# An encoder block on one Trainium2 core: values and output gate computed as eight pairs by seven products, x split tile by tile, row squares, and a hand-written order up to the first pair

## The chip, the cores and the metric

The kernel runs on one core of a Trainium2 chip. The time is the device time of one execution in microseconds (us); the number given for a kernel is the median of several runs. The trace that is quoted comes from one further execution under the hardware profiler.

## What is computed

One trunk layer of a hybrid encoder, in float32, for 2048 positions of width 1024. Only the first part matters here:

```python
xn = rms_norm(h, ln_mix_g)                 # h = x, (2048, 1024)
proj = xn @ w_in                           # (2048, 2512): q k v o | gates cq ckv kr
q_pre, k_pre = proj[:, 0:512], proj[:, 512:1024]
v_pre, o_pre = proj[:, 1024:1536], proj[:, 1536:2048]
rest = proj[:, 2048:2512]                  # 16 gates, 256 cq, 128 ckv, 64 kr
qk = silu(dwconv3_centred(q_pre | k_pre))  # along the 2048 positions
y_a = sigmoid(o_pre) * rms_norm(mlstm(q, k, v_pre, gates))
y_b = mla(rms_norm(cq), rms_norm(ckv), rope(kr))
h = h + concat(y_a, y_b) @ w_out           # then a gated MLP and an embedding gate
```

The row factor of the first norm, 1/sqrt(mean(x*x)+eps), is applied to the products and not to x; the gain is multiplied into the weights.

## The kernel before

Each float32 product is made of three matmuls on "fp32r" parts. An operand is split into a high part (a cast on ScalarE, ACT) and a low part (operand minus high part, on VectorE, DVE; `split`, L117), and a product is low*high + high*low + high*high (`mm3`, L131). A matmul of 128 rows by 512 columns over 1024 inputs is thus 8 blocks of 128 inputs times 3, 24 matmuls.

`in_proj` (L176) does the projections in three stages, and fills `x`-tiles, sixteen places of 16 KB per partition that hold the split x for all of them.

- **Rest** (the last 464 columns). For each of 16 tiles of 128 positions: load the tile of x (already turned, so that inputs lie on partitions), split it into its place (`split_x`), square it (ACT, L231), add the squares on DVE (L233, L234) and sum over partitions by two small matmuls with a column of ones (L237); GpSimd (POOL) raises that to -1/2 (L240), which gives the tile's row factor `rcol`. Then come 24 matmuls of 464 columns (`nat`), and in `rest` the results are scaled, normed and turned by the rotary table on DVE and ACT, and stored; two tiles later `turn_rest` transposes them on TensorE (PE, L281) and ACT copies the result out (L283).
- **Values and output gate.** Weights for 512 columns are loaded and split, then 16 tiles of 24 matmuls of 512 columns; the same again for the gate (L324 to L342). `gates()` is a generator of small steps, one of which is taken after each tile.
- **q and k** (`block`, L379): eight groups of 128 columns, four blocks of 512 positions each, 24 matmuls a block. The x parts are already in their places. A second generator, `side` (`absorb`, `q_up`), is advanced by `pump` three or four times a block, 0.986 steps a call. In this stage the order on PE is that of the program (`manual_schedule`); all other orders are made by a scheduler that knows costs.

Later stages already use pairs: two tiles of the left operand are taken together, both operands are cut into 2 by 2 blocks, and seven products of half the depth (12 matmuls each) take the place of eight (Winograd's form). `prep_a` and `prep_b` make the left sides of a pair from two loaded tiles: A11 and A12 (one split of 1024 columns), A22 (one of 512), four sums and differences of 512 on DVE, and two more splits of 1024 for S1, S3 and S2, S4. `OPX` names the places of the right sides B11, T1, T2, B21, T3, T4, B22.

Places in on-chip memory are named tags with one buffer each (`at`): a new tile under a tag waits until every reader of the old one is done. PSUM tags: `sc` has four banks, `tr` two, `pv` (the transposed rest tiles) one, `ml` one. Loads and stores are issued in order by one engine (SP).

Of the kernel before, what the change touches and what calls it, by code (L numbers as in the profile page):

```python
# [19 lines left out]
P = 128  # L20
S = 2048
# [15 lines left out]
LAG_T, LAG_X, LAG_R = 1, 2, 2  # L37
# [23 lines left out]
class Block:  # L61
# [114 lines left out]
    def in_proj(self):  # L176
        nc, d = self.nc, self.d
        xh = [[self.at(f"x{4 * c + 2 * f}", [P, 4, 512], F32R, f"xh{c}{f}") for f in range(2)] for c in range(4)]
        xl = [[self.at(f"x{4 * c + 2 * f + 1}", [P, 4, 512], F32R, f"xl{c}{f}") for f in range(2)] for c in range(4)]
        wrot, rrot, trot, srot = _rot("w", (*range(9), 13)), _rot("w", range(9, 13)), _rot("t", range(4)), _rot("s", range(3))  # L180
        w_in = d["w_in"][0].rearrange("(a b p) c -> a p b c", b=2, p=P)

        def load_w(c0, n, before=None):

            out, raws = [], []

            def load(k2, parts=1):
                raw = self.at(next(rrot), [P, 2, 512], name="wraw")
                for i in range(parts):
                    bs = slice(2 * i // parts, 2 * (i + 1) // parts)  # L190
                    nc.sync.dma_start(raw[:, bs, :n], w_in[k2, :, bs, c0:c0 + n])
                raws.append(raw)
                return raw

            if before:
                load(0, 2)
                before(0)
                load(1, 2)
                before(1)
                load(2)  # L200
                load(3)
            for k2 in range(KT // 2):
                if k2 == len(raws):
                    load(k2)
                raw = raws[k2]
                for b in range(2):
                    w = self.at(next(wrot), [P, 2, 512], F32R, "wsp")
                    self.split_g(raw[:, b, :n], gcol[:, 2 * k2 + b:2 * k2 + b + 1], w[:, 0, :n], w[:, 1, :n])
                    out.append(w)
            return out  # L210

        def nat(st, ws, n):
            ps = self.bank()
            c, o = st // 4, (st % 4) * P
            for kt in range(KT):
                f, k = divmod(kt, 4)
                self.mm3(ps[:, :n], xh[c][f][:, k, o:o + P], xl[c][f][:, k, o:o + P],
                         ws[kt][:, 0, :n], ws[kt][:, 1, :n], kt == 0, kt == KT - 1)
            return ps

        def load_x(st):

            t = self.at(next(rrot) if st else "u2", [P, KT, P], name="x_t")
            if st:
                nc.sync.dma_start(t, d["x_turned"][:, :, st * P:(st + 1) * P])
            return t

        def ssq_x(st, x_t):

            sq = self.at("w13", [P, KT, P], name="x_sq")  # L230
            nc.scalar.activation(sq, x_t, AF.Square)  # L231
            ss = self.at("t7", [P, 4, P], name="x_ss")
            nc.vector.tensor_tensor(ss, sq[:, 0:4], sq[:, 4:8], op=ALU.add)  # L233
            nc.vector.tensor_tensor(ss[:, 0:2], ss[:, 0:2], ss[:, 2:4], op=ALU.add)  # L234
            ps = self.pml.tile([P, 4], F32, name="ssp", tag="ml")
            for i in range(2):
                nc.tensor.matmul(ps, ss[:, i], ones, start=i == 0, stop=i == 1)  # L237
            t = self.stat(1, "rsm")
            nc.vector.tensor_scalar(t, ps[:, 0:1], 1.0 / D, EPS, op0=ALU.mult, op1=ALU.add)
            nc.gpsimd.tensor_tensor(rcol[:, st:st + 1], t, self.nhalf[:, :1], op=ALU.pow)  # L240

        def split_x(st, x_t):
            c, o = st // 4, (st % 4) * P
            for f in range(2):
                self.split(x_t[:, 4 * f:4 * f + 4], xh[c][f][:, :, o:o + P], xl[c][f][:, :, o:o + P])


        def rest(st):
            ps = nat(st, ws, NREST)
            rx = rcol[:, st:st + 1]  # L250
# [7 lines left out]
            cos, sin, tt = sc[:, 0], sc[:, 1], sc[:, 2:6]  # L258
# [5 lines left out]
            r = self.rsq(ssq, 2, 1.0)  # L264
            nc.vector.scalar_tensor_tensor(nn[:, 0:256], rs[:, 0:256], r[:, 0:1], gn[:, 0:256], op0=ALU.mult, op1=ALU.mult)
            nc.vector.scalar_tensor_tensor(nn[:, 256:384], rs[:, 256:384], r[:, 1:2], gn[:, 256:384], op0=ALU.mult, op1=ALU.mult)
            nc.sync.dma_start(self.vv_d[:, st], nn[:, 256:384])
            x1, x2 = rs[:, 384:416], rs[:, 416:448]
            nc.vector.tensor_tensor(tt[:, 0, :], x1, cos, op=ALU.mult)
            nc.vector.tensor_tensor(tt[:, 1, :], x2, sin, op=ALU.mult)  # L270
            nc.vector.tensor_tensor(tt[:, 2, :], x2, cos, op=ALU.mult)
            nc.vector.tensor_tensor(tt[:, 3, :], x1, sin, op=ALU.mult)
            nc.vector.tensor_tensor(nn[:, 384:416], tt[:, 0, :], tt[:, 1, :], op=ALU.subtract)
            nc.vector.tensor_tensor(nn[:, 416:448], tt[:, 2, :], tt[:, 3, :], op=ALU.add)
            nc.vector.tensor_copy(nn[:, 448:512], nn[:, 384:448])
            return nn

        def turn_rest(st, nn):
            pt = self.ppv.tile([P, 4, P], F32, name="rtp", tag="pv")
            for j in range(4):  # L280
                nc.tensor.transpose(pt[:, j, :], nn[:, j * P:(j + 1) * P], self.ident)  # L281
            rt = self.at(f"u{st % 2}", [P, 4, P], name="rt")
            nc.scalar.copy(rt, pt)  # L283
# [3 lines left out]
        nc.sync.dma_start(gcol, d["g_turned"])  # L287
# [3 lines left out]
        nq, xq = {}, {}  # L291

        xq[0] = load_x(0)

        def first(f):

            fs = slice(4 * f, 4 * f + 4)
            if f < 2:
                nc.sync.dma_start(xq[0][:, fs], d["x_turned"][:, fs, 0:P])
                self.split(xq[0][:, fs], xh[0][f][:, :, 0:P], xl[0][f][:, :, 0:P])  # L300

        ws = load_w(OFF_R, NREST, first)
        for st in range(NT + LAG_X):
            if st + 1 < NT:
                xq[st + 1] = load_x(st + 1)
            if st == 0:
                gn = self.at("t5", [P, 384], name="gn")
                self.row_bcast(gn[:, 0:256], d["q_norm_g"][0], 256)
                self.row_bcast(gn[:, 256:384], d["kv_norm_g"][0], 128)
                bg = self.row_bcast(self.cst.tile([P, 16], F32, name="bg"), d["b_gates"][0], 16)  # L310
            if 1 <= st < NT:
                split_x(st, xq[st])
            if 0 <= st - 1 < NT:
                ssq_x(st - 1, xq.pop(st - 1))
            if 0 <= st - LAG_X < NT:
                nq[st - LAG_X] = rest(st - LAG_X)
            if 0 <= st - LAG_X - LAG_R < NT:
                turn_rest(st - LAG_X - LAG_R, nq.pop(st - LAG_X - LAG_R))

        nc.sync.dma_start(self.r_d.rearrange("(t p) -> p t", p=P), rcol)  # L320
        gates = self.gates()

        ws = load_w(OFF_V, 512)
        for st in range(NT):  # L324
            ps = nat(st, ws, 512)
            if st < LAG_R:
                turn_rest(NT - LAG_R + st, nq.pop(NT - LAG_R + st))
            t = self.at(next(trot), [P, 512], name="vo")
            nc.vector.tensor_scalar(t, ps, rcol[:, st:st + 1], None, op0=ALU.mult)
            nc.sync.dma_start(self.v_d[st], t)  # L330
            if st >= LAG_R:
                next(gates, None)

        ws = load_w(OFF_O, 512)
        go = self.row_bcast(self.at("t6", [P, 512], name="go"), d["mlstm_norm_g"][0], 512)
        for st in range(NT):
            ps = nat(st, ws, 512)
            t = self.at(next(trot), [P, 512], name="vo")
            nc.scalar.activation(t, ps, AF.Sigmoid, scale=rcol[:, st:st + 1])
            nc.vector.tensor_tensor(t, t, go, op=ALU.mult)  # L340
            nc.sync.dma_start(self.o_d[st], t)
            next(gates, None)  # L342
        for _ in gates:
            pass

        cw = self.at("w13", [32, P], name="cw")
        nc.sync.dma_start(cw[0:24], d["conv_qk_w"][0].rearrange("t (j p) -> (t j) p", p=P))
        nc.sync.dma_start(cw[24:32], d["conv_qk_b"][0].rearrange("(j p) -> j p", p=P))
        pc = self.tbank([P, 32])
        nc.tensor.transpose(pc, cw, self.ident[:32, :32])  # L350
        cwt = self.cst.tile([P, 4, 8], F32, name="cwt")
        nc.vector.tensor_copy(cwt.rearrange("p a b -> p (a b)"), pc)
        H = S // 2
# [1689 lines left out]
```

## Time and profile before

| what | us |
|---|---|
| median of 3 runs (2891.49 to 2894.02) | 2893.66 |
| the profiled execution's own time | 2899.36 |
| its span, first to last instruction | 2897.6 |
| first matmul of the rest stage | 7.48 |
| first matmul of the values | 106.56 |
| first matmul of q and k | 283.26 |

The page of the profile lists the busy time of each engine; in a timeline a row has the start, the time covered, the engine, the line, the operation, its tiles and shapes, and in brackets the idle time before it with what ended it. In a table of groups "| busy us, mean ns |" follow the count. Matmuls overlap: the mean duration of one is longer than the distance between two starts, and it is the distance that counts.

### The profile page before, as it was taken

The numbers are of one execution on the slowest core, as the hardware profiler recorded it, in microseconds if no ns is written. First come the engines' busy times: TensorE is split into PE (matmuls) and PEld (weight loads), VectorE is DVE, ScalarE is ACT, GpSimd is POOL, SyncE is SP. The second block draws the span as 40 slices with busy tenths as digits, with TensorE's granted clock in tenths as the row PEclk, the third lists the DMA queues.
The fourth block names the chain that finished last, engine by engine and source line by source line (L and its number), as shares of the span: only waits on it lengthen the run. The fifth ranks groups of instructions, "written<-read, shape, count | busy, mean of one in ns | idle before, by whom it ended". The sixth has DMA issues, their size and how long they took to land. (4 is left out here: it accounts for less than half of the span.)

```text
span 2897.6 us, 40196 instructions
## 1 busy us (share of the span) xinstructions
PE 2851.3 (98%) x14110; PEld 2389.4 (82%) x14110; DVE 2045.3 (71%) x3790; ACT 1506.4 (52%) x2998; POOL 209.6 (7%) x311
## 2 busy tenths in 40 slices
PE   8999999999999999999999999999999999999998
PEld 7888888788888888778788888788888788888787
DVE  7521556777777777776777877867777867676787
ACT  7311544556666666655655555655556433254765
POOL 3100000000000010024300000000000000002111
PEclk9999999999999999999999999999999999999999
DMA  6512545643333233378844554657676757476764
GB/s 188 132 59 76 163 126 162 218 155 116 112 106 104 97 106 112 124 237 274 275 142 167 191 176 142 217 180 234 226 237 211 240 181 260 157 261 213 267 219 163
DMA packets 408315, 508.94 MB, mean 176 GB/s; under 512 B 34081, under 2 KB 271665, under 8 KB 408113
## 3 DMA queue, kind: packets, MB, share of 16 engines
q1 hardware_dynamic: 408112, 506.37, 53.9%
q8 instruction: 111, 1.82, 0.2%
q14 instruction: 92, 0.75, 0.1%
HBM read 324.16 MB, written 182.12 MB: 175 GB/s over the span
## 5 line engine op out<-in xcount | busy, mean ns | idle before, releaser
L1435 PE MATMUL fz<-op,fw 128*128 128x512 f32 x1968 | 477.2, 391 | 3.4 <-ACT fw L120 3.4
L1435 PE MATMUL fy<-op,fw 128*128 128x512 f32 x1968 | 475.4, 390 | 1.5 <-ACT fy L1547 1.5
L1435 PE MATMUL fx<-op,fw 128*128 128x512 f32 x1968 | 476.0, 390 | 0.0
L1435 PEld LDWEIGHTS fz<-op,fw 128*128 128x128 f32 x1968 | 367.4, 188 | 80.4 <-ACT fw L120 4.2
L1435 PEld LDWEIGHTS fy<-op,fw 128*128 128x128 f32 x1968 | 368.5, 188 | 78.5 <-ACT fy L1547 2.2
L1435 PEld LDWEIGHTS fx<-op,fw 128*128 128x128 f32 x1968 | 368.1, 188 | 76.1 <-ACT fy L1547 0.2
L1435 PE MATMUL fy<-op,fwd 128*128 128x512 f32 (+1 forms) x984 | 238.2, 390 | 3.4 <-DVE uv L1420 3.4
L120 ACT CAST pt<-tb 128x512 fp32r<-128x512 f32 x256 | 147.0, 586 | 173.2 <-PE tb L977 172.4
L133 PE MATMUL bk<-wsp,xh 128*128 128x512 f32 (+1 forms) x768 | 234.6, 386 | 0.0
L1435 PEld LDWEIGHTS fy<-op,fwd 128*128 128x128 f32 x984 | 182.7, 188 | 42.3 <-DVE uv L1420 4.9
L919 DVE TENSOR_REDUCE mx<-bk 128x1 f32<-128x512 f32 x256 | 174.6, 684 | 41.9 <-PE bk L918 40.9
L123 DVE TENSOR_TENSOR pt<-tb,pt 128x512 fp32r<-128x512 f32 x256 | 174.0, 683 | 31.0 <-ACT pt L120 29.3
L937 ACT ACTIVATE pe<-bk,nm 128x512 f32<-128x512 f32 x256 | 174.6, 695 | 38.1 <-DVE nm L931 33.6
L989 PE MATMUL ppv<-pt,kv 128*128 128x512 f32 x512 | 189.1, 407 | 0.5 <-DVE pt L123 0.5
L133 PEld LDWEIGHTS bk<-wsp,xh 128*128 128x128 f32 x768 | 145.6, 190 | 25.2
L133 PE MATMUL bk<-wsp,xl 128*128 128x512 f32 (+1 forms) x384 | 150.8, 393 | 7.5 <-DVE xl L123 7.5
L133 PE MATMUL bk<-xh,wqk 128*128 128x512 f32 x480 | 157.2, 393 | 0.0
L977 PE MATMUL tb<-ident,pe 128*128 128x128 f32 x1024 | 151.2, 274 | 4.1 <-DVE pt L123 3.6
L990 PE MATMUL ppv<-pt,kv 128*128 128x256 f32 x512 | 145.1, 283 | 0.0
L977 PEld LDWEIGHTS tb<-ident,pe 128*128 128x128 f32 x1024 | 122.5, 141 | 24.6 <-DVE pt L123 6.5
L120 ACT CAST fw<-hraw 128x1024 fp32r<-128x1024 f32 (+1 forms) x72 | 70.2, 981 | 117.1 <-PE fx L1435 58.9
L120 ACT CAST op<-opr 128x512 fp32r<-128x512 f32 x165 | 96.0, 621 | 65.2 <-DMA opr<-tw_d 16.6
(363 smaller groups left out, 5163.0 us busy)
## 6 DMA issues: line engine op xcount, KB each, us to landing
fwr<-in_w_up SPq DMA_DIRECT2D x66, 512.0 KB, 5.4
fh<-h_d SPq DMA_DIRECT2D x48, 512.0 KB, 3.7
h_d<-fh SPq DMA_DIRECT2D x48, 512.0 KB, 4.0
s_d<-fwr SPq DMA_DIRECT2D x44, 512.0 KB, 2.6
fws<-s_d SPq DMA_DIRECT2D x44, 512.0 KB, 3.6
rw<-row_d SPq DMA_DIRECT2D x32, 512.0 KB, 5.0
tw_d<-tsum SPq DMA_DIRECT2D x60, 256.0 KB, 5.1
opr<-tw_d SPq DMA_DIRECT2D x60, 256.0 KB, 4.8
```

What stands on the lines that cost most here:

```text
L120: nc.scalar.copy(hi, src)
L123: (sub or nc.vector).tensor_tensor(lo, src, _f(hi), op=ALU.subtract)
L133: mm = lambda *a, **k: self.nc.tensor.matmul(*a, **k, skip_group_check=more)
L919: nc.vector.tensor_reduce(s.mx[:, kb:kb + 1], ps, axis=AX.X, op=ALU.max)
L937: nc.scalar.activation(s.pe[:, kb % 2], s.banks[kb], AF.Exp, bias=s.nm, scale=ASCALE, accum_out=s.rs[:, kb:kb + 1])
L977: nc.tensor.transpose(t[:, j, :], s.p[kb][:, j * P:(j + 1) * P], self.ident)
L989: mm(w.ps, vh[:, ks], pts[kb][:, j], start=kt == 0, stop=False, skip_group_check=True)
L990: mm(w.ps[:, 0], vl[:, ks], pts[kb][:, j, 0], start=False, stop=kt == NT - 1, skip_group_check=True)
L1435: nc.tensor.matmul(out, a[:, k * P:(k + 1) * P], parts[lo][:, cols], start=first, stop=lo == 1 and k == last, skip_group_check=more)
```

## The change

The seven products replace the two loops for values and gate: a pair takes two tiles of 128 positions, the two halves of the 1024 inputs, and values and gate as the two column blocks. T1, T2, T3, T4 are sums of the weight blocks, made by `vo_sums` and `vo_late` in steps between the rest tiles. Since the places now hold those right sides, x isn't kept: it is loaded and split per tile for the rest stage, loaded again for the pairs (`load_pair`, `prep_a`, `prep_b`), and a third time for q and k (`load_qx`, through three staging places). The first four rest tiles are computed together, input block by input block (`first_block`). From the fifth tile on the squares come from rows of x, loaded besides, by one ACT instruction with an accumulated sum. Eight matmuls on the identity stand at the start. PE, DVE and ACT follow the order of the program until the first pair's end. The first group of q and k takes its blocks in the order 0, 3, 1, 2 with the last pair's remaining products between, and the side steps start later and run faster.

```diff
+        def square(st):
+            t, ss = rows.pop(st), self.stat(1, "x_ss")
+            nc.scalar.activation(t, t, AF.Square, accum_out=ss)
+            self.rsq(ss, 1, 1.0 / D, rcol[:, st:st + 1])
...
+        def first_block():
...
+            for kt in range(KT):
...
+                self.split_g(raws[kt // 2][:, kt % 2, :NREST], gcol[:, kt:kt + 1], w[:, 0, :NREST], w[:, 1, :NREST])
+                self.split(xr[kt], x[:, 0], x[:, 1])
+                for n, (a, e) in enumerate(((0, 0), (1, 0), (0, 1))):
+                    for st in range(4):
+                        nc.tensor.matmul(ps[st][:, :NREST], x[:, a, st * P:(st + 1) * P], w[:, e, :NREST],
+                                         start=kt == 0 and n == 0, stop=kt == KT - 1 and n == 2)
+                if kt:
+                    sq = self.at(f"u{kt % 2}", [P, 512], name="x_q")
+                    nc.scalar.activation(sq, xr[kt], AF.Square)
+                    tt(acc, acc, sq, op=ALU.add)
...
         def rest(st):
-            ps = nat(st, ws, NREST)
-            rx = rcol[:, st:st + 1]
+            ps, rx = done.pop(st), rcol[:, st:st + 1]
...
             rs = self.at(f"t{st % 2}", [P, 448], name="rs")
...
+            part.append((st, rs, sc, nn, self.rsq(ssq, 2, 1.0)))
+        def normed():
+            st, rs, sc, nn, r = part.pop(0)
...
+            stt(nn[:, 0:256], rs[:, 0:256], r[:, 0:1], gn[:, 0:256], op0=ALU.mult, op1=ALU.mult)
...
+            full.append((st, nn))
+        def turn_rest():
+            st, nn = full.pop(0)
             pt = self.ppv.tile([P, 4, P], F32, name="rtp", tag="pv")
...
+        def take_turned(act=False):
+            st, pt = turned.pop(0)
+            rt = self.at(next(urot), [P, 4, P], name="rt")
+            (nc.scalar.copy if act else nc.vector.tensor_copy)(rt, pt)
...
+        def vo_sums():
+            for k in range(4):
...
+                nc.scalar.activation(r0, r0, AF.Copy, scale=g1)
+                self.split(r0, *vo_place("B11", k))
+                yield
+                stt(r1, r1, g1, r0, op0=ALU.mult, op1=ALU.subtract)
+                self.split(r1, *vo_place("T1", k))
+                yield
+                stt(r1, r3, g2, r1, op0=ALU.mult, op1=ALU.subtract)
+                self.split(r1, *vo_place("T2", k))
+                yield
+                tt(r0, r1, r0, op=ALU.subtract)
+                yield
...
+        take = {4: (0,), 5: (1, 2), 6: (3,), 7: (4, 5), 8: (6,), 9: (7, 8), **{st: (st - 1,) for st in range(10, NT)}}
+        with self.tc.manual_schedule(engines=order):
+            for _ in range(8):
+                nc.tensor.matmul(wp, self.ident, self.ident, start=True, stop=True)
+            ps, acc = first_block()
...
+            for st in range(4, NT):
+                if turned:
+                    take_turned()
+                if len(full) > 1:
+                    turn_rest()
+                done[st] = nat(st)
+                if st + 2 < NT:
+                    split_x(st + 2)
+                if st + 3 < NT:
+                    load_x(st + 3)
+                if turned:
+                    take_turned()
+                for _ in range(len(part)):
+                    normed()
+                for i in take[st]:
+                    rest(i)
+                square(st)
...
+                some(sums, {6: 1, 7: 1, 9: 1, 15: 1}.get(st, 2 if st > 7 else 0))
+                if 10 < st < 15:
+                    some(late, 1)
...
+                if st == 14:
+                    prep = chain(self.prep_a(VO), self.prep_b(VO))
+                    some(prep, 1)
+                if st == 15:
+                    some(prep, 3)
+                if full:
+                    turn_rest()
...
-        ws = load_w(OFF_V, 512)
-        for st in range(NT):
-            ps = nat(st, ws, 512)
...
+        def load_qx(c, f):
+            hi, lo = [self.at(f"x{4 * c + 2 * f + e}", [P, 4, 512], F32R, f"x{'hl'[e]}{c}{f}") for e in range(2)]
...
+            for i in range(2):
+                ks = slice(2 * i, 2 * i + 2)
+                raw = self.at(next(qrot), [P, 2, 512], name="qxr")
+                nc.sync.dma_start(raw, d["x_turned"][:, 4 * f + 2 * i:4 * f + 2 * i + 2, c * 512:(c + 1) * 512])
+                self.split(raw, hi[:, ks], lo[:, ks])
...
+        for p in range(1, NT // 2):
...
+            prod(x, s.ops["A11"], "B11")
+            nc.scalar.copy(s.y, x)
+            if p == last:
+                load_qx(0, 0)
+            prod(s.z, s.ops["S1"], "T1")
...
+            rest_y(prev)
...
+            prod(s.y, s.ops["S2"], "T2", True)
...
+            prod(x, s.ops["A12"], "B21", True)
+            values(2 * p, x)
+            rest_z(prev)
...
+            prod(s.y, s.ops["S3"], "T3", True)
...
-        due = [0.0]
+        due, made = [-11.0], set()
         def pump():
-            due[0] += 0.986
+            due[0] += 1.16
...
+                if j == 0:
+                    block(0, 0, self.bank)
+                    rest_y(prev)
+                    load_qx(1, 0)
+                    rest_z(prev)
+                    load_qx(2, 0)
+                    wqk[1] = load_qk(1)
+                    block(0, 3, self.bank)
+                    block(0, 1, self.bank)
+                    conv(0, 0)
+                    block(0, 2, self.bank)
```

In `absorb` a pause goes from 5 to 3 steps and another from 2 to 4 for three of four heads.

More of the change, by code (lines that the diff above doesn't have):

```diff
@@ L181, in in_proj @@
+        urot = chain((f"{u}" for _ in range(5) for u in ("u0", "u1", "t7")), ("u0", "u1"))
         w_in = d["w_in"][0].rearrange("(a b p) c -> a p b c", b=2, p=P)
[L183 to L210, printed above, removed]
@@ L219, in nat @@
             return ps
         def load_x(st):
[L223 to L240, printed above, removed]
@@ new lines, in in_proj, with prod @@
+        go = self.row_bcast(self.at("t6", [P, 512], name="go"), d["mlstm_norm_g"][0], 512)
+        gates = self.gates()
+        class Pair:
+            pass
+        def prod(out, w, x, more=False):
+            n = 0
+            for a, lo in ((0, 0), (1, 0), (0, 1)):
+                for k in range(4):
+                    nc.tensor.matmul(out, w[a][:, k * P:(k + 1) * P], vo[x][k][lo], start=not more and n == 0,
+                                     stop=n == 11, skip_group_check=more)
+                    n += 1
```

325 lines of the change are left out of this document (240 added, 85 removed).

## The prediction

> **What bounds the kernel now.** I read the page's busy shares first, then the busy time by stage, then the timeline of PE.
>
> ```profile
> span 2897.6 us, 40196 instructions
> ...
> PE 2851.3 (98%) x14110; PEld 2389.4 (82%) x14110; DVE 2045.3 (71%) x3790; ACT 1506.4 (52%) x2998; POOL 209.6 (7%) x311
> ```
>
> ```profile
> 0.00:20.00 20.00, 12.13 (x48) 10.48 (x49) 12.13 (x27) 13.25 (x20) 2.16 (x8) 1.00 0.91 263
> ...
> 7.40:104.00 96.60, 94.59 (x490) 84.27 (x491) 68.96 (x254) 64.60 (x145) 34.21 (x59) 1.00 0.67 170
> 104.00:283.30 179.30, 179.30 (x804) 148.22 (x803) 49.13 (x127) 27.11 (x52) 2.15 (x6) 1.00 0.24 74
> 283.30:509.00 225.70, 225.70 (x1150) 191.39 (x1149) 130.92 (x328) 100.86 (x194) 0.00 (x0) 1.00 0.51 153
> ```
>
> The columns are the busy us of PE, weight loads, DVE, ACT and POOL, then the granted clock, the DMA share and GB/s. PE is never idle in the stages of values and gate and of q and k; in the rest stage DVE is busy 71% and ACT 67%, in the value stage only 27% and 15%. So a matmul saved in the middle stage is time saved, as long as DVE and ACT bring the new operands. The busy time per matmul would mislead; the distance of starts counts:
>
> ```profile
> 106.20 0.60 PE L281 MATMUL rtp<-ident,nn 128*128 128x128 f32 x4
> 106.56 0.48 PE L133 MATMUL bk<-wsp,xl 128*128 128x512 f32 x1
> ...
> 281.90 0.39 PE L133 MATMUL bk<-wsp,xl 128*128 128x512 f32 x1
> ...
> 282.58 0.39 PE L133 MATMUL bk<-wsp,xl 128*128 128x512 f32 x1
> ...
> 283.26 0.39 PE L133 MATMUL bk<-xh,wqk 128*128 128x512 f32 x1
> ```
>
> Three matmuls of 512 columns take 0.68, one 0.227. The stage runs from 106.56 to 283.26, 176.7; its 768 matmuls are 174.1 of it, 2.6 are transposes. Four transposes of a rest tile cost 0.36.
>
> ```profile
> 7.48 0.76 PE L133 MATMUL bk<-wsp,xl 128*128 128x464 f32 x1 [7.48 <-DVE xl L123]
> ...
> 10.35 0.97 PE L133 MATMUL bk<-wsp,xh 128*128 128x464 f32 x2
> 11.13 0.59 PE L133 MATMUL bk<-wsp,xl 128*128 128x464 f32 x1
> ...
> 13.28 0.38 PE L133 MATMUL bk<-wsp,xl 128*128 128x464 f32 x1
> ...
> 22.98 0.50 PE L237 MATMUL ssp<-ones,x_ss 128*128 128x4 f32 x4
> 23.34 0.45 PE L133 MATMUL bk<-wsp,xl 128*128 128x464 f32 x1
> ...
> 24.05 0.37 PE L133 MATMUL bk<-wsp,xl 128*128 128x464 f32 x1
> ...
> 24.68 0.37 PE L133 MATMUL bk<-wsp,xl 128*128 128x464 f32 x1
> ```
>
> A matmul of 464 columns takes 0.21, at the start 0.39 (two in 0.78 from 10.35), and a sum over ones 0.36 and more.
>
> **The change, part by part.**
>
> *PE alone.* 768 matmuls of 512 become 8 x 84 + 2 = 674: 94 x 0.227 = 21.3 saved. 16 sums over ones become one group: about 6 saved with their waits. The first product needs only the high parts, and the activation table (1.28, ahead of the first split) is loaded before the data come: the first matmul moves from 7.48 to about 5.5, and the eight matmuls on the identity spend part of the slow start (15 matmuls in 5.8 where 3.1 would do) earlier. PE by itself would run 5.5 + 1.5 (rest of the slow start) + 384 x 0.21 = 80.6, + 0.5 + 16 x 0.36 = 5.8, + 674 x 0.227 = 153, + 2.2: q and k would start at 249, **34 earlier** than 283.
>
> *DVE and ACT in the rest stage.* Now they must do it in the time that PE takes. Durations:
>
> ```profile
> L120 ACT CAST fw<-yr 128x1024 fp32r<-128x1024 f32 x24 | 25.1, 1052 | 28.0 <-PE fz L1435 8.3 <-PE fx L1435 7.0 <-DVE yr L1409 6.3
> L120 ACT CAST xh<-x_t 128x512 fp32r<-128x512 f32 x32 | 18.7, 614 | 8.4 <-DMA x_t<-in_x_turned 8.3
> L255 ACT ACTIVATE rs<-bk,rcol 128x448 f32<-128x448 f32 x16 | 10.2, 636 | 13.4 <-DVE rsm L239 10.2 <-DVE gt L252 3.2
> L261 ACT ACTIVATE nn<-rs 128x256 f32<-128x256 f32 x16 | 6.6, 411 | 0.0
> L262 ACT ACTIVATE nn<-rs 128x128 f32<-128x128 f32 x16 | 4.8, 298 | 0.0
> L1830 ACT ACTIVATE junk<-fh 128x1024 bf16<-128x1024 f32 x16 | 16.9, 1059 | 1.7 <-DVE fh L1420 1.7
> ```
>
> ```profile
> L123 DVE TENSOR_TENSOR fw<-yr,fw 128x1024 fp32r<-128x1024 f32 x24 | 29.7, 1239 | 1.4 <-ACT fw L120 1.3
> L129 DVE SCALAR_TENSOR_TENSOR wsp<-wraw,gcol,wsp 128x512 fp32r<-128x512 f32 x16 | 11.4, 747 | 0.7 <-ACT wsp L128 0.7
> L731 DVE COPY cols<-gps 128x128 f32<-128x128 f32 x2 | 0.6, 280 | 0.0
> L252 DVE SCALAR_TENSOR_TENSOR gt<-bk,rcol,bg 128x8 f32<-128x8 f32 x32 | 5.8, 223 | 2.0 <-PE bk L133 1.6 <-POOL rcol L240 0.4
> ```
>
> ```profile
> 69.67 0.19 DVE L269 TENSOR_TENSOR sc<-rs,sc 128x32 f32<-128x32 f32 x1
> ...
> 70.42 0.19 DVE L275 COPY nn<-nn 128x64 f32<-128x64 f32 x1
> ...
> 72.57 0.48 DVE L265 SCALAR_TENSOR_TENSOR nn<-rs,rsr,gn 128x256 f32<-128x256 f32 x1 [1.95 <-POOL rsr L143]
> ...
> 73.24 1.28 DVE L123 TENSOR_TENSOR xl<-x_t,xh 128x512 fp32r<-128x512 f32 x2
> ```
>
> Back to back an instruction costs a little under its duration: 0.64 for a DVE split of 512, so I take 1.19 for 1024 and 0.70 for a scaled sum. `normed` is 0.67 for its two scalings and about 0.73 for five small ones (seven take 0.95): 1.4. The copy of a transposed tile (`take_turned`) has no row; it lies between the 0.28 of 128 columns and the 0.75 of a scaled one. The 0.28 is mostly fixed, and I take 0.64, a pass over 512. The gate sums are 0.3 a tile. From tile 4 on, until the S operands of pair 0, DVE does 10 splits of x (11.9), 12 copies (7.7), 14 `normed` (19.6), 15 gate sums (4.5), the weight sums 4 x (3 splits + 2 scaled sums + 1 difference = 3.98) = 15.9, four low parts of B21 (2.8) and pair 0's operands (6.8): **69**. PE needs 288 x 0.21 + 12 x 0.36 = 65. ACT does, a tile, cast 1.02, rest 1.35, squares 1.17 and about 1.1 for weights: 4.6, 56 in all. So DVE is the bound of this stretch even if it never waits, and three waits are built in. (a) All transposed tiles share one PSUM bank, and the next transposes stand in PE's order ahead of the next tile's matmuls: PE waits for DVE's copy. (b) A result `rs` has two places, so ACT's scaling of tile i waits for `normed` of tile i-2, and the casts of weights queue behind it. (c) Each of eight weight sums goes DVE, ACT (cast, 0.6), DVE, with nothing between on DVE: 5 in all at least.
>
> I stepped through the order of the three engines with these durations, first block ending at 27. DVE ends the steps of tiles 5 to 14 at 35, 45, 52, 60, 70, 79, 85, 93, 99 and 107, and the S operands at **116**: 19 of waiting on 69 of work. PE waits before tile 9 from 54 to 60, before tile 11 from 71 to 79, and within pair 0 from 109 to 115 for ACT's copy of tile 12, queued behind pair 0's casts. Pair 0 ends at 127; T4 and B22 are split until 142; at 145 PE has done 134 of the 674 matmuls (30.4 of work in the 39 since tile 15). The other 540 x 0.227 = 122.4 and the 2.6 give 270. From here a pair takes PE 19; DVE has 11 and ACT 7 of work a pair, so they don't bind. The transposes of `gates` stand between the products and wait for DVE, which is no longer idle: 1.5. So q and k start at **271.5 instead of 283.3: 11.8 gained**, not 34.
>
> *x for q and k, again.* 16 loads of 512 KB pass three staging places. From the first free place to the last block of the first group PE has 168 matmuls, 38 us.
>
> ```profile
> x_t<-in_x_turned SPq DMA_DIRECT2D x15, 512.0 KB, 4.1
> ...
> rest_d<-rt SPq DMA_DIRECT2D x16, 256.0 KB, 6.6
> ```
>
> Landing 4.1, cast 1.05, split 1.24 and issue 0.5 make 6.9 a place; 13 loads behind the first three need 13/3 x 6.9 = 30: hidden. But with the other traffic (about 3 MB) it is 11.4 MB, and the first window above moved 263 GB/s at a share of 0.91, 289 full: 39.5. Between nothing and 13/3 x (9.4 - 6.9) = 11 at the other row's landing I take 2.5, near the rate. If that cover goes, each us of landing beyond 6.0 costs 4.3.
>
> *At nothing:* the later and faster side steps (109 calls' worth for 106 steps, before 102 for 102; ACT and DVE are busy 45% and 58% there; from a gain of 1 to a loss of 3), the store of the row factors through a transpose, the halo condition, the x rows (12 loads, two tiles ahead of use; 20 MB in 84 us, 242 GB/s, under 289; a wait would cost what it lasts, since DVE is the bound). The instruction order from the attention's start on is that of before, so no later stage changes.
>
> **Sum:** 11.8 - 2.5 = 9.3. The profiled execution took 2899.36, its span 2897.6; the median is 5.7 less, and the same step off it gives 2893.66 - 9 = **2884.7**.
>
> **Rivals.**
>
> *PE stays the bound.* If DVE and ACT overlap better than I stepped (the 19 of waiting go), q and k start up to 34 earlier: 2860; with half of it 2872. For: 69 against 65 is close. Against: (a) and (b) are in the order itself.
>
> *The clock falls back.* After 7.48 idle the trace shows 0.39 a matmul for 5.8 us, 2.7 lost. A short wait does no such thing:
>
> ```profile
> 517.76 0.50 PE L914 MATMUL bk<-kv,q_s 128*128 128x512 f32 x1 [1.78 <-ACT pe L937]
> 518.10 0.39 PE L915 MATMUL bk<-kr,q_t 128*128 128x512 f32 x1
> ```
>
> After 1.78 the distance is 0.34, then that of full speed. My three waits of 6 to 8 lie between these rows. If each brings the slow start back, up to 8 of the gain go: 2893, within 0.2%. DVE is late then anyway, which speaks for less. The Trainium skill, "TensorE: Matmul & The Clock Gate", section "What's actually happening", has such a rule: an idle window of about 3.4 us halves the clock until as long a busy one. By it each of the three would cost 1.7, an estimate from that page, 5 in all: 2890. No wait of before but the first is long enough to show it.
>
> *The staged x holds up q and k (slower).* Place: the first group's blocks 3, 1, 2. Price 4.3 for each us by which a load lands later than 6.0. It eats the gain at a landing of 8.7, and at 11 the time is 2903. For: two of the last three places come free only as DVE splits, stores stand between the loads in SP's order, and the needed rate is the top of what the trace shows. Against: 4.1 in the row of such loads.
>
> *That the products aren't saved* can be left out: the built order holds 674.
>
> **How the numbers follow.** My forecast, 2878 to 2888: 0.42. PE stays the bound, 2858 to 2878: 0.22. The clock, or another loss that leaves 2888 to 2899: 0.18. Slower, 2899.5 to 2912: 0.18. Faster by over 0.2% (5.8 us, about what a measurement of this kernel tells from no change): 0.42 + 0.22 = 0.64; within 0.18; slower 0.18. The range 2865 to 2904 leaves out some 0.06 below and 0.1 above; the likeliest case alone is 2878 to 2888.
>
> **What would show it.** First matmul of a product at 5 to 6; DVE over 80% busy from 30 to 115; PE waits on `rtp` for the copy `rt`, 5 us and more, near tiles 9 and 11; first pair at 106, its S product at 115; q and k at 268 to 274; after the fourth block the distances of before. Wrong: PE over 97% busy from 30 to 110 (then the gain is over 20), or waits on `xl` of the staged x over 5 us in the first group.

## The result, and the profile after

The changed kernel takes 2914.36 us in the median of 6 runs (2907.73 to 2917.04), the kernel before on the same chip 2894.88 (6 runs, 2891.49 to 2898.03). The ratio is 1.0061 with a 95% interval of 1.0051 to 1.0072: slower by 0.6%, some 19 us, where 9 less were forecast. The profiled execution took 2914.65. Times below are compared as ratios, since the kernel before took 2894.9 to 2899.3 on the chips of the several measurements.

First the page of the changed kernel, then three stretches of it: from the first block's end to the first pair, the pairs, and q and k to their last product.

```profile
span 2912.5 us, 40152 instructions
...
PE 2837.7 (97%) x13977; PEld 2375.5 (82%) x13977; DVE 2138.5 (73%) x3843; ACT 1572.6 (54%) x3083; POOL 203.8 (7%) x320
```

```profile
27.00:128.90 101.90, 73.07 (x336) 63.08 (x334) 59.13 (x168) 52.50 (x122) 28.03 (x65) 0.87 0.65 199
128.90:293.80 164.90, 155.46 (x680) 126.35 (x681) 121.53 (x225) 80.67 (x122) 3.41 (x8) 0.97 0.42 132
293.80:530.00 236.20, 233.40 (x1175) 197.01 (x1174) 145.01 (x344) 110.52 (x206) 0.00 (x0) 0.99 0.57 171
```

PE was busy 2851.3 us before and is busy 2837.7 now, with 133 matmuls fewer: the products that were to be saved are saved, though part of the rest now runs at a lower clock. The first row is where the time went. For 102 us PE is busy 72%, DVE 58% and ACT 52%: no engine binds this stage, which in the kernel before kept PE at 98%. The timeline of PE shows the waits:

```profile
68.68 1.12 PE L277 MATMUL rtp<-ident,nn 128*128 128x128 f32 x4 [8.76 <-DVE rt L283]
...
91.76 1.11 PE L277 MATMUL rtp<-ident,nn 128*128 128x128 f32 x4 [10.10 <-DVE rt L283]
...
111.93 5.27 PE L133 MATMUL bk<-wsp,xs 128*128 128x464 f32 x24
120.31 1.11 PE L277 MATMUL rtp<-ident,nn 128*128 128x128 f32 x4 [3.11 <-DVE rt L283]
121.08 7.69 PE L133 MATMUL bk<-wsp,xs 128*128 128x464 f32 x24
128.93 0.50 PE L493 MATMUL voy<-op,fw 128*128 128x512 f32 x1 [0.16 <-ACT fw L120]
...
140.93 1.12 PE L277 MATMUL rtp<-ident,nn 128*128 128x128 f32 x4 [8.17 <-ACT rt L283]
141.69 5.37 PE L436 MATMUL voz<-op,fw 128*128 128x512 f32 x12
...
293.79 0.39 PE L133 MATMUL bk<-xh,wqk 128*128 128x512 f32 x1
```

The first pair starts at 128.9, not 106, and its S product at 141.7, not 115. At 293.8 q and k begin with 24 of the 674 products still to come, so against the forecast of 271.5 they are 22 late and those 24 products (5.4) besides. The waits are named after `rt`, the copy of a transposed tile. That is the end of a chain and not its cause: DVE makes that copy in its order, and DVE is late. What DVE and ACT themselves wait for, from 20 to 130 (in total, times, longest):

```profile
DVE op L123 <- ACT op L120: 33.0, 12, 6.9
DVE xs L123 <- ACT xs L120: 6.3, 2, 3.6
```

```profile
ACT rs L250 <- DVE gt L247: 45.8, 11, 6.1
```

Each waits for the other. DVE wants the casts of ACT, and ACT's scaling of a result (`rs`, L250) wants the gate sums of DVE (`gt`, L247). One step of the two, ACT first and then DVE:

```profile
95.46 0.64 ACT L250 ACTIVATE rs<-bk,rcol 128x448 f32<-128x448 f32 x1 [4.13 <-DVE gt L247]
...
96.83 1.04 ACT L201 ACTIVATE x_n<-x_n 128x1024 f32<-128x1024 f32 x1
...
97.87 0.71 ACT L318 ACTIVATE vr<-vr,gcol 128x512 f32<-128x512 f32 x1
98.61 0.62 ACT L120 CAST op<-vr 128x512 fp32r<-128x512 f32 x1
99.14 0.72 ACT L128 ACTIVATE op<-vr,gcol 128x512 fp32r<-128x512 f32 x1
99.77 1.04 ACT L120 CAST xs<-x_t 128x1024 fp32r<-128x1024 f32 x1
104.26 0.63 ACT L250 ACTIVATE rs<-bk,rcol 128x448 f32<-128x448 f32 x1 [3.45 <-DVE gt L247]
```

```profile
95.01 0.36 DVE L247 SCALAR_TENSOR_TENSOR gt<-bk,rcol,bg 128x8 f32<-128x8 f32 x2
...
99.27 0.69 DVE L123 TENSOR_TENSOR op<-vr,op 128x512 fp32r<-128x512 f32 x1 [3.31 <-ACT op L120]
99.89 0.75 DVE L129 SCALAR_TENSOR_TENSOR op<-vr,gcol,op 128x512 fp32r<-128x512 f32 x1
100.56 0.68 DVE L283 COPY rt<-rtp 128x512 f32<-128x512 f32 x1
101.17 1.21 DVE L123 TENSOR_TENSOR xs<-x_t,xs 128x1024 fp32r<-128x1024 f32 x1
...
103.78 0.36 DVE L247 SCALAR_TENSOR_TENSOR gt<-bk,rcol,bg 128x8 f32<-128x8 f32 x2
```

ACT starts the scaling 0.1 after the second gate sum, then does the sums of squares, the squares of a row of x and the weight's scaling and cast; the moment the cast is done (99.23) DVE takes its low part, then the rest of its step, and comes to the next gate sums 8.77 after the last. Two more casts of ACT (at 99.14 and 99.77) fit beside DVE's work; apart from them, while one works the other stands. Why does ACT wait for `gt` at all? It does not read it. The two read one PSUM bank: the 16 gate columns and the 448 others are one result. The Trainium skill, "PSUM — Partial Sum Buffer", section "PSUM bank collisions raise a hardware error", says that two engines on one bank and quarter of the partitions at once raise an error, two reads included, and that the compiler's scheduler puts a dependency between such accesses. The trace agrees: 45.8 us of such waits by an engine that only reads, and a start 0.1 after the other's end. Which part of the tool chain puts the order in here, the runs don't show.

### The profile page after: what moved, and what is told of

It reads as the page before. It is cut to its first block, busy times and chain, and to the rows that moved or that the text cites. A ratio compares the mean times of both kernels' runs of the same rounds, so it can differ in the third digit from the quotient of the medians.

```text
span 2912.5 us, 40152 instructions
## 1 busy us (share of the span) xinstructions
PE 2837.7 (97%) x13977; PEld 2375.5 (82%) x13977; DVE 2138.5 (73%) x3843; ACT 1572.6 (54%) x3083; POOL 203.8 (7%) x320
## 4 chain that ended last, share of the span: by engine, by line
PE 81%; DVE 7%; ACT 5%; DMA 4%; issue 3%; POOL 1%; SPq 0%; POOLq 0%; ACTq 0%; DVEq 0%
PE fy L1669 21%; PE fz L1669 14%; PE fx L1669 14%; PE bk L133 4%; PE ppv L1223 3%; PE tb L1211 3%; PE voy L436 2%; PE bk L1148 2%; PE bk L1149 2%; PE bk L1150 2%; PE bk L1151 2%; PE bk L1152 2%; PE ppv L1224 2%; PE fs L133 1%; PE voz L436 1%
## 5 line engine op out<-in xcount | busy, mean ns | idle before, releaser
L133 PE MATMUL bk<-xh,wqk 128*128 128x512 f32 x480 | 157.0, 393 | 0.0
L123 DVE TENSOR_TENSOR fw<-fwr,fw 128x1024 fp32r<-128x1024 f32 x88 | 107.4, 1220 | 24.8 <-ACT fw L120 24.8
L1717 DVE SCALAR_TENSOR_TENSOR fgv<-uv,fcw,fgv 128x1024 f32<-128x1024 f32 x88 | 112.8, 1281 | 17.4 <-ACT fgv L1715 16.6
L123 DVE TENSOR_TENSOR op<-opr,op 128x512 fp32r<-128x512 f32 x165 | 108.5, 694 | 21.2 <-ACT op L120 21.0
```

What stands on the lines that cost most here:

```text
L123: (sub or nc.vector).tensor_tensor(lo, src, _f(hi), op=ALU.subtract)
L133: mm = lambda *a, **k: self.nc.tensor.matmul(*a, **k, skip_group_check=more)
L1717: nc.vector.scalar_tensor_tensor(t, u[:, tap:tap + 2 * SB], self.taps[:, tap, ct:ct + 1], t, op0=ALU.mult, op1=ALU.add)
```

## The experiments

**Theory A** is this loop: gate sums, scaling, casts, low part, split, `normed`, gate sums. **B**: the one PSUM bank of the transposed tiles, which PE's waits name. **C**: the clock, which falls in these waits. **D**, my prediction's view: DVE's work.

**e1. The gate sums first.**

```diff
             for st in range(4, NT):
+                for i in take[st]:
+                    gate_sums(i)
                 if turned:
                     take_turned()
```

`rest` no longer has them. Expected:

> Only the two gate sums of a tile move on DVE, from behind `normed` to the start of the step. Theory A (a loop between DVE and ACT): ACT's scaling of a result waits for the gate sums of that tile, and the gate sums stand behind DVE's work that waits for ACT's casts. In the trace the loop of one step is 8.8 us: on ACT scaling and two sums of squares 1.37, squares of a row of x 1.04, scaling and cast of a weight 1.36; then on DVE low part 0.62, scaled sum 0.67, copy of the transposed tile 0.61, split of x 1.13, `normed` 1.48, gate sums 0.36. With the gate sums first it is 1.37 + 1.04 + 1.36 + 0.62 + 0.67 + 0.27 = 5.3, so the ten steps from tile 6 on take 5.5 to 6.5, bounded by PE's 5.4: pair 0 starts at 97 to 108 instead of 129, the waits on `rtp` fall below 12 us from 37, and the time is 2882 to 2894. Theory B (one PSUM bank for the transposed tiles): the copy of the tile stands where it stood, 2910 to 2916. Theory C (the halved clock is most of it): the long waits stay or go with A; alone it says nothing here. Theory D (DVE is the bound by its work, as I predicted): pair 0 not before 112.

Measured: 1.0002 (0.9992 to 1.0011), so the whole loss of 0.6% is gone; A's 2882 to 2894, which is 0.9956 to 0.9997 of the kernel before, is just missed. The timeline of PE:

```profile
62.98 1.11 PE L280 MATMUL rtp<-ident,nn 128*128 128x128 f32 x4 [7.80 <-DVE rt L286]
...
85.84 1.11 PE L280 MATMUL rtp<-ident,nn 128*128 128x128 f32 x4 [8.83 <-DVE rt L286]
...
93.02 5.26 PE L133 MATMUL bk<-wsp,xs 128*128 128x464 f32 x24
...
98.47 5.26 PE L133 MATMUL bk<-wsp,xs 128*128 128x464 f32 x24
...
114.58 0.50 PE L498 MATMUL voy<-op,fw 128*128 128x512 f32 x1
```

From 93 on PE runs a tile in 5.45 (98.47 - 93.02) without a wait: there PE binds, as the rival of the prediction had it. Two long waits are left (7.80 and 8.83); with the short ones and one for ACT's copy in pair 0 it is 23 us on `rtp`, where less than 12 was expected. The first pair starts at 114.6, 14 earlier but outside the expected 97 to 108. So A holds, and something else stands behind it. D falls as the cause of the loss: with hardly any of DVE's work changed, the stage is 14 shorter, and DVE is busy 68% of what is left (59.6 of 87.6 from 27 on). D's sign, a first pair not before 112, did come here; in e10 below, with the same work on DVE, it comes at 105.6.

**e13. The place of the gate sums kept, the shared bank taken away.** This is the mechanism by itself:

```diff
-            for i, o in ((0, st), (8, NT - 1 - st)):
-                nc.vector.scalar_tensor_tensor(self.gt[:, i:i + 8, o], ps[:, i:i + 8], rx, bg[:, i:i + 8],
-                                               op0=ALU.mult, op1=ALU.add)
-            rs = self.at(f"t{st % 2}", [P, 448], name="rs")
-            nc.scalar.activation(rs, ps[:, 16:NREST], AF.Copy, scale=rx)
+            ra = self.at(f"t{st % 2}", [P, NREST], name="rs")
+            nc.scalar.activation(ra, ps[:, 0:NREST], AF.Copy, scale=rx)
+            rs = ra[:, 16:NREST]
+            for i, o in ((0, st), (8, NT - 1 - st)):
+                tt(self.gt[:, i:i + 8, o], ra[:, i:i + 8], bg[:, i:i + 8], op=ALU.add)
```

> The order of the changed kernel stays: the gate sums stand behind `normed`. Only what they read is another: ACT scales all 464 columns of a result into the place of `rs`, and DVE adds the gate bias from there, so DVE no longer reads the PSUM bank that ACT reads, and ACT's scaling no longer waits for the gate sums. Theory A in its exact form (the loop is closed by two engines reading one bank in program order, not by where the gate sums stand): ACT's waits for `gt`, 46 us between 20 and 130, are gone, the waits on `rtp` fall to 25 or less from 37, and the time falls as with the gate sums moved, 11 to 20 us, ratio 0.999 to 1.0025. If it is the place of the gate sums in DVE's order that costs (DVE late with something behind them), the ratio stays at 1.005 to 1.007.

Measured: 0.9991 (0.9982 to 1.0001). What ACT's scaling waits for now, and PE:

```profile
ACT rs L247 <- DVE nn L269: 12.7, 6, 3.1
ACT rs L247 <- POOL rcol L387: 5.0, 1, 5.0
```

```profile
PE rtp L277 <- DVE rt L283: 15.6, 3, 8.2
PE rtp L277 <- ACT rt L283: 5.1, 1, 5.1
```

The wait for `gt` is gone with the order on each engine untouched (L247 is now the scaling itself; DVE's gate sums now wait for it, 3.4 us in all). The first pair starts at 113.5. The shared bank is thus shown to be the cause: it alone is worth 0.7%. What comes up in its place is `nn`, the `normed` of two tiles before, which frees one of the two places of `rs`.

**e3. One member taken out of the loop.** `square(st)` moved ahead of `normed` and `rest`, so that ACT does it while it would wait:

```diff
+                square(st)
                 for _ in range(len(part)):
                     normed()
                 for i in take[st]:
                     rest(i)
-                square(st)
```

> The changed kernel with the squares of a row of x (1.04 us, with the read of the sum) ahead of the scaling of the result on ACT, and nothing else. Theory A (the loop of 8.8 us through gate sums, scaling, casts, low part, split, `normed`): 1.04 leaves the loop and is done while ACT waits, so ten steps give 8 to 10 us: ratio to before 1.0025 to 1.004 instead of 1.0061. If the loop is not what sets the pace (ACT waits anyway, and DVE's own work or the bank does), the ratio stays at 1.005 to 1.007.

Measured: 1.0028 (1.0016 to 1.0040). The loop foretells the size as well as the sign. Gate sums of tiles 3 and 14, nine steps apart, in the changed kernel and here:

```profile
45.03 0.36 DVE L247 SCALAR_TENSOR_TENSOR gt<-bk,rcol,bg 128x8 f32<-128x8 f32 x2
...
132.13 0.36 DVE L247 SCALAR_TENSOR_TENSOR gt<-bk,rcol,bg 128x8 f32<-128x8 f32 x2
```

```profile
44.88 0.36 DVE L247 SCALAR_TENSOR_TENSOR gt<-bk,rcol,bg 128x8 f32<-128x8 f32 x2
...
122.83 0.36 DVE L247 SCALAR_TENSOR_TENSOR gt<-bk,rcol,bg 128x8 f32<-128x8 f32 x2
```

87.1 / 9 = 9.68 a step, and 77.95 / 9 = 8.66: 1.02 less, for 1.04 taken out. (These are means: the steps of the changed kernel differ in what they hold and take 7.7 to 12.8.)

**e2. The low parts of the weight sums one step later** (`vo_sums` casts on ACT, yields, and takes the low part after the next resumption):

```diff
-                self.split(r1, *vo_place("T1", k))
+                b = vo_place("T1", k)
+                nc.scalar.copy(b[0], r1)
                 yield
+                low(r1, *b)
```

> The low part of each weight sum of V and O is taken on DVE one step after ACT's cast, so DVE finds the cast done. Theory A: the loop through the gate sums stays; low part and scaled sum (1.29) leave it and ACT's cast of x (1.04) with the wait for it comes in: about 7.8 us a step instead of 8.8, ten steps, 2903 to 2908. Rival (the round trips of the weight sums themselves are the cost; DVE waited 35 us for ACT's casts of them in the first 150 us): 2880 to 2892.

Measured: 1.0053 (1.0038 to 1.0068). The rival falls, but of the 10 us that A gave at most a part came; the interval does not part e2 from the changed kernel. I had overlooked that `vo_late` puts a weight of B21 into the steps of tiles 11 to 14, whose low part (L129) waits for its cast as before; and in the other steps the split of x takes the place: DVE waited 18.4 us for casts of x in it, 6.3 in the changed kernel.

**e4. Two banks for the transposed tiles 5 to 13.**

```diff
+            if 4 < st < 14:
+                pt = self.ptr.tile([P, 4, P], F32, name="rtp", tag="tr")
+            else:
+                pt = self.ppv.tile([P, 4, P], F32, name="rtp", tag="pv")
-            pt = self.ppv.tile([P, 4, P], F32, name="rtp", tag="pv")
```

> The transposed tiles 5 to 13 use the two PSUM banks of the other transposes, so PE no longer waits for the copy of the tile before. Theory A: PE runs ahead by a tile, but DVE and ACT go on at 8.8 us a step, and pair 0 waits for its operands: within 3 us of the changed kernel, 2911 to 2917, and PE's wait moves to the split of x (`xs`) or to pair 0's operand. Theory B (the single bank is the cost, 36 us of PE's waits stand there): 2885 to 2900.

Measured: 1.0053 (1.0038 to 1.0068), 2913.84 us. What PE waits for in it, up to 150:

```profile
PE rtp L280 <- DVE rt L286: 15.9, 4, 8.6
PE rtp L280 <- DVE nn L268: 7.0, 4, 3.9
PE voy L496 <- ACT fw L120: 6.7, 1, 6.7
PE voz L439 <- ACT rt L286: 5.9, 1, 5.9
```

The bank that the waits named was widened, and the same 35 us of waiting spread over other names. While the loop is closed, B is worth nothing that shows.

**e5. Work for PE while it waits.** 14 matmuls on x and weights already split, result unused, behind each of the tiles 7 to 15:

```diff
+                if st > 6:
+                    fp = self.pml.tile([P, 512], F32, name="fill", tag="ml")
+                    for n in range(14):
+                        nc.tensor.matmul(fp[:, :NREST], ws[0][:, 0, :P], ws[1][:, 0, :NREST], start=True, stop=True)
```

> 14 more matmuls of 464 columns (0.21 each, 2.9 a step, result unused) from tile 7 to 15, on PE behind each tile's product and ahead of its transposes, where PE waits 3 to 10 us. Theory A: the loop of 8.8 us a step stays, so only the products that end the stage get shorter, the last tile's (7.7 instead of 5.3) and the S product of pair 0 (5.4 instead of 2.9): 2908 to 2915. Theory C (the clock fell to 0.57 to 0.9 between 60 and 150, and that is most of the loss): granted clock above 0.95 there and 2895 to 2904. Both expect the clock to rise; a clock that stays low with the idle time cut to 6 us a step leaves C open.

Measured: 1.0062 (1.0046 to 1.0079). From 110 to 140, first the changed kernel, then this one:

```profile
110.00:140.00 30.00, 18.21 (x75) 14.63 (x73) 20.34 (x49) 15.19 (x33) 6.42 (x15) 0.83 0.36 106
```

```profile
110.00:140.00 30.00, 30.00 (x151) 26.91 (x150) 19.37 (x50) 15.56 (x34) 6.42 (x15) 1.00 0.32 92
```

The granted clock is full and PE is never idle, and DVE and ACT go no faster than they did beside a slow PE: from tile to tile, 11 to 14, the gate sums follow each other at 10.22, 7.67 and 10.50 us (at 110.25, 120.47, 128.14 and 138.64), in the changed kernel at 10.22, 7.66 and 10.47 (at 103.78, 114.00, 121.66 and 132.13). C as the main cause falls. What the fallen clock costs by itself is not settled by this, since the added matmuls took time of their own. The rows of PE give an estimate: behind the four waits with a lower clock the tiles, transposes and the product of pair 0 took some 9 us more in the changed kernel than at full speed, and in e13, which keeps three such waits, still some 6.4. So of the 18.5 by which e13's S product comes earlier (123.2 for 141.7), some 3 can be the clock.

**e7, e8, e6: what stands behind the loop.** Gate sums first with two banks (e7), with the squares ahead too (e8), and with the later low parts as well (e6).

> Gate sums first, and the transposed tiles 5 to 13 in the two PSUM banks of the other transposes. With the gate sums first, PE still waited 7.8 us at 55 to 63 and 8.8 at 77 to 86, both at transposes whose single bank the copy on DVE had not yet freed; outside these two it ran a tile in 5.46. Theory E (with the loop open, the single bank is the next limit): most of these 16.6 go, q and k start 8 to 15 earlier than the 277 with the gate sums alone, and the time is 0.3 to 0.5% under the kernel before. Theory F (the two places of `rs` are: ACT waited 14.3 for `normed` of the tile two before): PE waits as long for the split of x or for `normed`, and the time stays within 4 us of the gate sums alone, which was 1.0002 of before.

> As the run with gate sums first and two banks, and the squares of a row of x stand on ACT ahead of the scaling of the result, where ACT waits for DVE (1.2 us a tile). Theory E: where DVE and ACT still bind, up to 1.0 a step on some six steps, 3 to 6 us under the run without. Theory F: ACT's wait for `normed` of two tiles before only gets shorter by the same 1.0 and nothing is gained, within 2 us.

> Gate sums first, two banks, squares ahead of the scaling, and the low parts of the weight sums one step later. With the loop open the low parts no longer wait on a cast that itself waits for the gate sums; DVE's remaining waits for casts of weights were 21 us with gate sums first. Theory E: these waits lie beside PE's 5.46 a tile from 86 on, so at most 3 us under the run without the later low parts, or none. Rival (DVE's waits for the weights' casts still set the pace): 6 us or more.

Measured: e7 0.9988 (0.9978 to 0.9997), e8 0.9979 (0.9970 to 0.9988), e6 0.9979 (0.9970 to 0.9989). Against e1 the two banks are worth some 0.14% here, at the edge of what the intervals tell apart, where e4 gave 0.08%: by the times alone the two do not differ. The 4 us lie at the limit that F set. In the profiled executions q and k start 5.0 earlier in e7 than in e1 (272.2 for 277.2), less than E's 8 to 15; in e4 they start 1.7 earlier than in the changed kernel (292.1 for 293.8). With the squares ahead (e8) the medians are 3 us lower (2892.25 and 2889.15), the size E had, but the intervals overlap, and in the profiled executions q and k start at 272.2 in both: that the squares give these 3 us is not shown. The later low parts add nothing.

**e9 and e12. The side steps later, with and without the rest.**

```diff
-        due, made = [-11.0], set()
+        due, made = [-15.0], set()
```

> As the run before it, and the side steps beside q and k begin four blocks of pumping later (-15 for -11). In the changed kernel PE waits 2.4 us at 332 to 335 for the cast of `woa`, which stands on ACT behind the weights of q and k whose load landed late among the staged x, and the granted clock falls to 0.71 for 5 us: 4 us in all. If that is the transfers of the staged x, the later start takes 2 to 4 us off; if it is the side steps' own chain, the wait only moves and nothing is gained, or up to 3 are lost because the steps left over run in one piece at the end of block 6.

> The changed kernel with the side steps beside q and k begun later (-15 for -11), and nothing else. It gave 4 us (0.9964 against 0.9979) on top of gate sums, banks and squares. If the price is that of the staged x in the same stage, it is the same here: ratio 1.004 to 1.0055 and no wait on `woa`. If it came with the earlier stage's other timing, 1.0055 to 1.007.

e9: 0.9964 (0.9951 to 0.9976); its runs (2883.03 to 2885.78) lie all below those of e8 (2885.92 to 2892.99). e12: 1.0049 (1.0034 to 1.0064), about the same 4 us, though its interval alone does not part it from 1.0061. The changed kernel between 330 and 340, where PE waits for `woa`, and PE's waits from 290 to 520 in the changed kernel and in e12:

```profile
330.00:335.00 5.00, 2.70 (x11) 1.69 (x9) 4.39 (x10) 4.42 (x9) 0.00 (x0) 0.95 0.62 195
335.00:340.00 5.00, 4.99 (x16) 4.02 (x17) 1.80 (x4) 2.09 (x4) 0.00 (x0) 0.71 1.04 317
```

```profile
PE gb L133 <- ACT woa L120: 1.6, 1, 1.6
PE gb L133 <- DVE woa L123: 0.8, 1, 0.8
PE bk L133 <- DVE xl L123: 0.4, 1, 0.4
```

```profile
PE bk L133 <- DVE xl L123: 0.8, 1, 0.8
```

The waits on `woa` are gone, and with them the clock's dip (1.00 from 330 to 340 in e12).

**e10. The transposed tiles 1 and 3 in one more bank** (tag `ml`), on top of e9.

> The fastest so far (gate sums first, squares ahead, two banks, later side steps; 0.9964 of before) with the transposed tiles 1 and 3 in a fourth PSUM bank. In it PE still waits 7.2 us at 56 to 63 for the copy of tile 3 or 2 on DVE, and the tile behind takes 6.9 instead of 5.3 at a granted clock of 0.6. Theory E (bank): these 7 to 9 go on PE, but the end of the stage is set by pair 0's operands, so 2 to 6 us off the time, 0.9945 to 0.996. Theory F (DVE and ACT set the pace there too): the wait moves, 0.996 to 0.997.

Measured: 0.9953 (0.9937 to 0.9970), 2882.71 us in the median. The ratio lies in E's range, but its interval reaches into F's. The trace favours E: the first pair starts at 105.6 and q and k at 266.3 with 24 products still to come, each some 5 earlier than in e9 (110.5 and 271.1). That is near what was forecast for the change itself (106, and 271.5 with none to come). This version is faster than both kernels.

## Why the prediction was wrong

**The work: right.** On PE 674 products' matmuls in place of 768 and full-speed distances in the pairs; the first product came at 4.78, a little before the forecast's 5 to 6. The 249 of PE alone is not tested: in no run is PE without waits up to q and k. On DVE 69 us were forecast from the first block to pair 0's S operands, and DVE is busy 69.0 from 27 to 141.6, where the last of them is done. In e10 q and k start at 266.3 with 24 products (5.4) to come, 271.7 in the forecast's terms and 11.5 earlier than before: a gain of the forecast's size was there to be had. That it agrees with the 11.8 is partly luck, since e10 is the change with five more edits and has other waits than those forecast.

**The waiting of DVE: the step that failed.** I stepped the three engines through their order, put 19 us of waiting on the 69 of work, and so 8 us a step. Measured from 27 to 141.6 is 45.6 of waiting beside the 69.0. The ends of DVE's steps 5 to 14, forecast and as the timeline of DVE has them:

| step | 5 | 6 | 7 | 8 | 9 | 10 | 11 | 12 | 13 | 14 |
|---|---|---|---|---|---|---|---|---|---|---|
| forecast | 35 | 45 | 52 | 60 | 70 | 79 | 85 | 93 | 99 | 107 |
| measured | 36 | 50 | 59 | 68 | 80 | 91 | 101 | 111 | 120 | 130 |

The start is right and the slope is wrong: 10.4 a step, not 8. I had listed three built-in waits and missed the fourth, ACT's scaling behind DVE's gate sums. The row for it stood in my own quotation: "13.4 <-DVE rsm L239 10.2 <-DVE gt L252 3.2". In the kernel before it cost 3.2, because the gate sums came early enough there for two of them to wait for PE ("2.0 <-PE bk L133 1.6"); in the new order they stand behind `normed`. I had put that wait at nothing. With it the order of two engines is a ring, and then most of their durations add up instead of overlapping. DVE was to be over 80% busy from 30 to 115; it is 59%.

**The three waits that I had.** (a), the single bank, was of the right kind and before the right tiles, 9 and 11 (8.76 until 68.7 and 10.10 until 91.8; forecast 6 until 60 and 8 until 79). It mostly passed the delay on: e4, with two banks, lies within its interval of the changed kernel. (b), two places of `rs`, comes out only when the ring is open: 14.3 us in e1, 12.7 in e13. (c), the round trips of the weights, I put at "5 in all at least"; DVE waited 33.0 for those casts. A third to a half of it comes of the ring, in which each cast stands on ACT behind a scaling that waits for DVE: with the ring open 20.3 (e1) and 16.4 (e13) are left.

**The copy of tile 12 behind pair 0's casts:** forecast 6 of waiting, measured 8.17; right in kind.

**The clock falls back:** it did, behind three of the waits before tiles and once in pair 0 (7.69 for a tile of 5.27, 5.37 for a product of 2.9). I gave this a chance as a reason for a smaller gain, up to 8; some 9 came, by the estimate under e5, which also shows that it is not the main reason for the loss.

**x staged for q and k:** forecast 2.5, with 11 as the far end, through waits on `xl`. Those were 0.4. The stage is 4.5 longer all the same: it ends at 529.7 after 293.8, less 5.4 of products, where before it took 225.9. The price came through `woa`, a side step whose cast queues on ACT behind the weights of q and k; that the staged x's transfers made those late is argued from the DMA share and not shown by itself.

**Later stages:** instructions in the same order, and no wait of PE over 1 us that the kernel before did not have too. From the first product of the attention on (493.6 before, 514.1 now) the profiled execution takes 5.6 less than that of before. Of that, 4.5 is that the profiled execution of before lay above its median (2899.36 for 2894.88), so it is not read as a gain.

**The sum.** From a gain of 9.3 to a loss of 19.5 it is 28.8: 26.7 up to the S product of pair 0 (141.7 for 115), as much as DVE waited beyond the forecast (45.6 for 19), 1 more up to the start of q and k (22.3 and the 5.4 of products still to come), and 2 in q and k (4.5 for 2.5). That these make 0.9 too many is within the spread of single executions. The chance of 0.18 for slower stood on another mechanism; the range ended at 2904.

## What to carry to other kernels

Where several engines follow an order written by hand, don't add up their work: draw for one step who waits for whom, and look for a ring; its length, not the busiest engine, is the time of a step. Reads count: in this kernel two engines that read one PSUM bank followed each other in program order, so let one of them read the bank out (e13), or put the small read first (e1). And a wait names the last link only; widening that brought q and k 1.7 earlier while the ring was closed (e4) and 5.0 once it was open (e7), by single profiled executions.

## What the runs showed of the hardware

**A wait shorter than the forecast's mark can be followed by the slow pitch.** I had 1.78 (no effect) and 7.48. In the changed kernel 3.11 was enough (7.69 for the tile behind it). In e10 PE waited twice, nearly as long:

```profile
57.18 0.63 PE L285 MATMUL rtp<-ident,nn 128*128 128x128 f32 x4 [2.15 <-DVE nn L271]
57.56 6.84 PE L133 MATMUL bk<-wsp,xs 128*128 128x464 f32 x24
...
72.69 0.63 PE L285 MATMUL rtp<-ident,nn 128*128 128x128 f32 x4 [2.38 <-DVE nn L271]
73.07 5.26 PE L133 MATMUL bk<-wsp,xs 128*128 128x464 f32 x24
```

The shorter wait made the tile behind it 1.6 longer, the longer one did nothing. The Trainium skill, "TensorE: Matmul & The Clock Gate", section "What's actually happening", speaks of about 3.4 us of an idle window that runs freely; that it does not start with the wait agrees with the two rows, but that 2.15 was enough does not follow from it. Counting the four transposes ahead of each wait and the four behind it, which may or may not hold the clock up (no run shows it), 3.1 and 3.4 us lie between the products' matmuls (54.43 to 57.56 and 69.71 to 73.07).

**The transfers were faster than I took for full.** From 30 to 40 the changed kernel moves 369 GB/s where I had worked out 289 for full, and PE has no wait in it:

```profile
30.00:40.00 10.00, 10.00 (x51) 8.94 (x50) 3.88 (x13) 6.85 (x21) 3.90 (x11) 1.00 1.07 369
```
